# The Strassen output projection of a gated hybrid encoder step: vector and scalar work kept in written order, a third weight slot, six gate buffers

## The chip, the core and the metric

The kernel runs on one core of one Trainium2 chip. The metric is device time in microseconds (us) of one launch. Beside the plain runs stands one profiled execution, whose trace gives every duration below: when each engine started and ended each instruction, and what released it. Engines are named as the profile names them: PE (TensorE matmul) with PEld (its weight loads), DVE (VectorE), ACT (ScalarE), POOL (GpSimd) and SP (the engine that issues the transfers). A "q" behind an engine's name is its sequencer.

## What is computed

One layer of a streaming encoder for 1024 prompt frames and 32 sample frames (1056 columns together, 1024 channels). What matters here is the end of it:

```
ya  = (o_attn * silu(ga)) @ w_pa
yb  = (silu(layernorm(conv)) * silu(gb)) @ w_pb
m   = sigmoid(ma) * ya + sigmoid(mb) * yb
out = x + m @ w_out
```

All products are wanted in full float32. The kernel splits each operand into a rounded high part and the remainder (`wh`, `wl` for weights, `mh`, `ml` for `m`), and adds three matmuls: high by high, low by high, high by low.

## The kernel before

The data lie with channels on the 128 partitions and frames along the free dimension, so a weight of 1024 x 1024 is eight tiles of 128 output channels, each of 8 x 128 x 128 numbers. The program has these stages in order: projections of the input, attention with the gate projections filled in between its blocks, the product with `w_pa` ("pa"), the product with `w_pb` ("pb"), and the output projection with `w_out`.

**A weight** is fetched by `load_raw` (L88, 512 KB, three buffers taken in turn in pa and pb), and split by `split_w`: ACT writes the high part (L94), POOL subtracts it in three pieces to get the low part (L97). `wh` and `wl` have two slots each, in the pool `wp`. One weight feeds 72 matmuls of 352 columns (L105).

**The stage pa** takes, for each of the eight output tiles, three gate tiles `sma` of 352 columns: a transfer reads each (L1173), ACT applies tanh (L1174), DVE multiplies it with the matmul's result from the accumulator (L1177), and a transfer writes it to `s_ya` (L1178). The pool `sg2` has four buffers for them. Between the tiles, `ln_out` (L1127 to L1138) prepares the other branch.

**The stage pb** reads `s_mb` and `s_ya` back, applies tanh (L1215), evaluates (L1220, L1221) and splits `m` (ACT L1224, POOL L1225). In between `form_sums` builds, out of the quarters of `m`, the sums that Strassen's product takes (DVE, L1200 to L1203), and `halves_to` splits them (ACT L1193, DVE L1194).

**The output projection** handles output tiles in four pairs, the frames in two halves of 528 columns (`L`, `R`), and the contraction in two halves of four tiles. Each pair has seven products, each of 24 matmuls of 264 columns (L1290): two in `first`, with the plain weight, and five in `second`, with the weight sums `sa` and `sb` and a plain quarter `z`. All four `first` come before all four `second`. The weight sums are made from two raw weights per pair (DVE L1270, L1271 for `sa`, L1275, L1276 for `sb`, one buffer each) and split by `w_tile` (ACT L1249, POOL L1253, two slots in `wp` and two in `op`). Results leave the accumulator (eight banks, two for a product) by ACT (`u`, L1311) or DVE (`u` L1322, `v` L1325, outputs L1300), are combined with the residual `x` (L1312, L1321), and stored (L1301). The pool `op`, with two of the four weight slots and `tfs[1]`, lies where pb's operands `c_h` and `c_l` lay.

**Order.** From the attention on, only PE keeps the order in which the program is written:

```
es.enter_context(tc.manual_schedule(engines={E.PE}))
```

Instructions of the other engines are ordered by a planner with its own estimate of times, and `tc.high_priority(offset=...)` moves what stands inside ahead. Every engine then works through its list in order, and an instruction that waits holds up all that stand behind it. In the earliest stages DVE and ACT are in the written order too; there `later(n, fn)` puts work at a place n beats ahead, and `beat()` counts a beat and issues what is due.

Of the kernel before, what the change touches and what calls it, by code (L numbers as in the profile page):

```python
# [51 lines left out]
def build(tc, xT, xt, wv, wf, ckT, cv, clT, stT, vec, cst, yT, kT, vO, lfO, cpT, csT):  # L52
# [4 lines left out]
    def pool(name, bufs=1, stack=es, **kw):  # L57
        return stack.enter_context(tc.tile_pool(name=name, bufs=bufs, reuse_waits="tile", **kw))
# [18 lines left out]
    mean = lnp.tile([128, TT], F32, name="mean")  # L77
    rstd = lnp.tile([128, TT], F32, name="rstd")
    rawp = [wp]

    def f32(ap):
        return ap.bitcast(F32)

    def load_raw(key, offset=2000):
        with tc.high_priority(offset=offset):
            rawp.append(rawp.pop(0))
            raw = rawp[-1].tile([128, KT, 128], F32, name="raw", tag="raw", bufs=1)
            nc.sync.dma_start(raw, wf[WIDX[key]])  # L88
        return raw

    def split_w(raw, offset=2000):
        with tc.high_priority(offset=offset):
            wh = wp.tile([128, KT, 128], F32R, name="wh", tag="wh")
            nc.scalar.copy(wh, raw)  # L94
            wl = wp.tile([128, KT, 128], F32R, name="wl", tag="wl")
            for k0, k1 in WSP:
                nc.gpsimd.tensor_sub(wl[:, k0:k1, :], raw[:, k0:k1, :], f32(wh[:, k0:k1, :]))  # L97
        return wh, wl
# [157 lines left out]
    def sums(f):  # L256
        return [lambda: from_shift(f, sides["y", f]), lambda: into_sums(f, sides["y", f])]
# [571 lines left out]
    pps.close()  # L829


    es.enter_context(tc.manual_schedule(engines={E.PE}))
# [355 lines left out]
    L, R = slice(0, HT), slice(HT, TT)  # L1188
    mixed = {}
    parts = {}  # L1190

    def halves_to(h, l, t):
        nc.scalar.copy(h, t)  # L1193
        nc.vector.tensor_sub(l, t, f32(h))  # L1194

    def form_sums(j):
        a, b = mixed.pop(j), mixed.pop(j + 4)
        t, u = (mean, rstd) if j < 3 else (big("t3"), big("u3"))
        V = nc.vector
        V.tensor_sub(t[:, L], a[:, R], a[:, L])  # L1200
        V.tensor_sub(u[:, L], b[:, R], a[:, R])
        V.tensor_sub(t[:, R], b[:, R], t[:, L])
        V.tensor_sub(u[:, R], b[:, L], t[:, R])  # L1203
        halves_to(mh[:, j, R], ml[:, j, R], u[:, L])
        parts[j] = t[:, R], t[:, L], u[:, R]

    def form_halves(j):
        for i, t in enumerate(parts.pop(j)):
            tf = tfs[j // 2]
            halves_to(tf[:, i, 0, j % 2, :], tf[:, i, 1, j % 2, :], t)  # L1210

    def mk_pb(f):
        smb = mixed[f] = big("smb")
# [14 lines left out]
    def formed(f):  # L1228
        for j in range(3):
            if PBO.index(f) == 2 * j + 2:  # L1230
                form_sums(j)
                if j < 2:
                    form_halves(j)
# [5 lines left out]
    rawp.append(op)  # L1239
    tfs.append(op.tile([128, 3, 2, 2, HT], F32R, name="tf"))  # L1240
    homes = [op, op, wp, wp]
    form_halves(2)
    form_sums(3)
    form_halves(3)

    def w_tile(src, n=2):
        homes.append(homes.pop(0))
        wh, wl = [homes[-1].tile([128, KT, 128], F32R, name=a, tag=a, bufs=2) for a in ("wh", "wl")]
        nc.scalar.copy(wh[:, :4 * n, :], src)  # L1249
        for k0, k1 in WSP:  # L1250
            k1 = min(k1, 4 * n)
            if k1 > k0:
                nc.gpsimd.tensor_sub(wl[:, k0:k1, :], src[:, k0:k1, :], f32(wh[:, k0:k1, :]))  # L1253
        return wh, wl

    class Pair:


        def __init__(self, p):
            self.p = p  # L1260
            self.u = op.tile([128, HT], F32, name=f"u{p}")
            self.w = [None] * 3

        def made(self, i):
            V = nc.vector
            with tc.high_priority(offset=2000):
                if i == 0:
                    self.r = [load_raw(("out", 2 * self.p + n), 0) for n in range(2)]
                    sa = self.sa = op.tile([128, KT, 128], F32, name="sa", tag="sa", bufs=1)
                    V.tensor_add(sa[:, 4:, :], self.r[1][:, :4, :], self.r[1][:, 4:, :])  # L1270
                    V.tensor_sub(sa[:, :4, :], sa[:, 4:, :], self.r[0][:, :4, :])  # L1271
                    self.w[0] = w_tile(sa)
                elif i == 1:
                    sb = op.tile([128, KT, 128], F32, name="sb", tag="sb", bufs=1)
                    V.tensor_sub(sb[:, :4, :], self.r[0][:, :4, :], self.r[1][:, :4, :])  # L1275
                    V.tensor_sub(sb[:, 4:, :], self.r[0][:, 4:, :], self.sa[:, :4, :])  # L1276
                    self.w[1] = w_tile(sb)
                else:
                    self.w[2] = w_tile(self.r[1][:, 4:, :], 1)

        def product(self, w, half, mov, evac, pss=None):
            wh, wl = w
            more = pss is not None
            pss = pss or [pjC.tile([128, CH], F32, name="pj", tag="pj") for _ in range(2)]
            for c in range(2):
                for kt in range(4):
                    h, l = [m(kt, slice(c * HC, c * HC + HC)) for m in mov]
                    k = 4 * half + kt
                    for n, (a, x) in enumerate(((wh, h), (wl, h), (wh, l))):
                        nc.tensor.matmul(pss[c][:, :HC], a[:, k, :], x, start=(not more and kt == 0 and n == 0),  # L1290
                                         stop=(kt == 3 and n == 2), skip_group_check=more)
# [15 lines left out]

        def first(self, w, x):
            u = self.u
            self.residual(0, 0, x)  # L1310
            self.product(w, 0, quad(0, L), lambda sl, ps: nc.scalar.copy(u[:, sl], ps))  # L1311
            nc.vector.scalar_tensor_tensor(x, u, 0.5, x, op0=ALU.mult, op1=ALU.add)  # L1312
            self.product(w, 1, quad(4, L), self.out(0, 0, x))

        def second(self, then):
            u, (sa, sb, z) = self.u, self.w
            t1, t2 = big("r1"), big("r2")
            x12, x21, x22, v = t1[:, L], t1[:, R], t2[:, L], t2[:, R]
            for x, m, hf in ((x12, 0, 1), (x21, 1, 0), (x22, 1, 1)):
                self.residual(m, hf, x)  # L1320
            half_of = lambda x, y: nc.vector.scalar_tensor_tensor(y, x, 0.5, y, op0=ALU.mult, op1=ALU.add)  # L1321
            self.product(sa, 0, form(0), lambda sl, ps: nc.vector.tensor_add(u[:, sl], u[:, sl], ps))  # L1322
            half_of(u, x21)
            half_of(u, x12)
            c = self.product(sa, 1, form(1), lambda sl, ps: nc.vector.tensor_add(v[:, sl], u[:, sl], ps))  # L1325
            half_of(v, x22)
            then(0)
            d = self.product(sb, 0, quad(0, R), self.out(1, 1, x22))
            self.product(sb, 1, quad(4, R), self.out(0, 1, x12), c)
            then(1)  # L1330
            self.product(self.w[2], 0, form(2), self.out(1, 0, x21), d)
            then(2)

    def quad(k0, cols):
        return [lambda kt, sl, m=m: m[:, k0 + kt, cols.start + sl.start:cols.start + sl.stop] for m in (mh, ml)]

    def form(i):
        return [lambda kt, sl, n=n: tfs[kt // 2][:, i, n, kt % 2, sl] for n in range(2)]

    pairs = [Pair(p) for p in range(4)]  # L1340
    for p in range(4):
        if p % 2 == 0:
            both = big("r0")
        w = w_next
        if p < 3:
            with tc.high_priority(offset=2000):
                w_next = w_tile(load_raw(("out", 2 * p + 2), 0))
        if p > 1:
            pairs[0].made(p - 2)
        pairs[p].first(w, both[:, (L, R)[p % 2]])  # L1350
    pairs[0].made(2)

    for p in range(4):
        def then(n):
            if n == 0 and p < 3:
                pairs[p + 1].made(0)
            elif n == 1 and p < 3:
                pairs[p + 1].made(1)
            elif n == 2 and p < 3:
                pairs[p + 1].made(2)  # L1360

        pairs[p].second(then)
    p3.close()
    es.close()

# [81 lines left out]
```

## Time and profile before

| what | value |
|---|---|
| runs of the kernel | 1391.44, 1391.41, 1389.38 us; median 1391.41 |
| the profiled execution, its own time | 1390.03 us |
| its span in the trace | 1388.2 us |
| outside the span | 1.8 us |
| mean clock granted to TensorE | 0.999 |
| PE busy | 1374.9 us |
| DVE, ACT, POOL busy | 975.4, 660.0, 653.3 us |

Busy time of PE is that of pipelined matmuls whose ends are modelled: consecutive ones overlap in the record, so their pace is read from their starts. "Idle before, released by" says how long an engine stood still before an instruction and which other engine's instruction ended that.

### The profile page before, as it was taken

The numbers are of one execution on the slowest core, as the hardware profiler recorded it, in microseconds if no ns is written. First come the engines' busy times: TensorE is split into PE (matmuls) and PEld (weight loads), VectorE is DVE, ScalarE is ACT, GpSimd is POOL, SyncE is SP. The second block draws the span as 40 slices with busy tenths as digits, with TensorE's granted clock in tenths as the row PEclk, the third lists the DMA queues.
The fourth block names the chain that finished last, engine by engine and source line by source line (L and its number), as shares of the span: only waits on it lengthen the run. The fifth ranks groups of instructions, "written<-read, shape, count | busy, mean of one in ns | idle before, by whom it ended". The sixth has DMA issues, their size and how long they took to land. (4 is left out here: it accounts for less than half of the span.)

```text
span 1388.2 us, 25134 instructions
## 1 busy us (share of the span) xinstructions
PE 1374.9 (99%) x9478; PEld 1336.3 (96%) x9478; DVE 975.4 (70%) x1368; ACT 660.0 (48%) x1346; POOL 653.3 (47%) x685
## 2 busy tenths in 40 slices
PE   9999999999999999999999999999999999999999
PEld 8999999999999999999999999999999999999999
DVE  6687788878898999647666766655555488156773
ACT  6433434656464642245555556655555566233320
POOL 2324244656575875443433343333433267255662
PEclk9999999999999999999999999999999999999999
DMA  5253442424242374245545556444642678534452
GB/s 213 63 173 123 147 144 92 155 75 160 94 163 88 118 205 152 92 135 136 150 127 164 144 158 178 126 138 139 175 133 88 234 276 272 176 120 144 146 174 69
DMA packets 113496, 203.36 MB, mean 146 GB/s; under 512 B 17696, under 2 KB 75936, under 8 KB 113376
## 3 DMA queue, kind: packets, MB, share of 16 engines
q1 hardware_dynamic: 113232, 201.70, 46.0%
q8 instruction: 75, 1.23, 0.4%
q14 instruction: 45, 0.37, 0.1%
q10 hardware_dynamic: 144, 0.07, 0.0%
HBM read 131.87 MB, written 69.84 MB: 145 GB/s over the span
## 5 line engine op out<-in xcount | busy, mean ns | idle before, releaser
L105 PE MATMUL pj<-xh,wh 128*128 128x352 f32 (+2 forms) x1536 | 509.7, 332 | 0.4 <-ACT t L776 0.3
L105 PE MATMUL pj<-xl,wh 128*128 128x352 f32 (+2 forms) x1536 | 494.9, 322 | 0.2
L105 PE MATMUL pj<-xh,wl 128*128 128x352 f32 (+2 forms) x1536 | 493.5, 321 | 0.0
L97 POOL TENSOR_TENSOR wl<-raw,wh 128x384 fp32r<-128x384 f32 (+1 forms) x237 | 307.5, 1325 | 185.7 <-ACT wh L94 163.2
L269 DVE SCALAR_TENSOR_TENSOR y<-u,vec_t,y 128x1086 f32<-128x1086 f32 x240 | 378.5, 1578 | 11.5 <-ACT y L266 8.3
L105 PEld LDWEIGHTS pj<-xh,wh 128*128 128x128 f32 x1536 | 289.4, 188 | 3.4 <-ACT xh L441 0.9
L105 PEld LDWEIGHTS pj<-xl,wh 128*128 128x128 f32 x1536 | 289.0, 188 | 1.0 <-DVE xl L442 1.0
L105 PEld LDWEIGHTS pj<-xh,wl 128*128 128x128 f32 x1536 | 289.8, 189 | 0.2 <-DVE wl L461 0.2
L954 POOL TENSOR_SCALAR P<-P,nm 128x128 f32<-128x128 f32 (+7 forms) x128 | 99.3, 776 | 230.1 <-DVE nm L953 206.0
L948 DVE TENSOR_REDUCE nm<-psS 128x1 f32<-128x128 f32 (+7 forms) x128 | 96.5, 755 | 72.5 <-PE psS L946 53.8
L975 ACT CAST pth<-ptr 128x512 fp32r<-128x512 f32 (+1 forms) x192 | 89.2, 482 | 80.7 <-PE ptr L971 80.3
L976 DVE TENSOR_TENSOR ptl<-ptr,pth 128x512 fp32r<-128x512 f32 (+1 forms) x192 | 103.4, 551 | 23.3 <-ACT pth L975 21.7
L951 ACT ACTIVATE P<-psS,nm 128x128 f32<-128x128 f32 (+7 forms) x128 | 95.4, 745 | 35.0 <-DVE nm L948 31.4
L94 ACT CAST wh<-raw 128x1024 fp32r<-128x1024 f32 x79 | 82.8, 1048 | 50.7 <-PE pj L105 21.6
L738 POOL TENSOR_TENSOR ql<-qn,qh 128x352 fp32r<-128x352 f32 (+1 forms) x48 | 64.5, 1343 | 68.9 <-ACT qh L737 59.9
L971 PE MATMUL ptr<-ident,P 128*128 128x128 f32 x576 | 85.0, 274 | 0.0
L987 PE MATMUL po<-pth,V 128*128 128x256 f32 x320 | 78.9, 282 | 0.0
L988 PE MATMUL po<-ptl,V 128*128 128x256 f32 x320 | 78.5, 281 | 0.0
L597 PE MATMUL pjv<-vwh,xh 128*128 128x260 f32 x256 | 72.5, 283 | 0.0
L597 PE MATMUL pjv<-vwl,xh 128*128 128x260 f32 x256 | 72.4, 283 | 0.0
L597 PE MATMUL pjv<-vwh,xl 128*128 128x260 f32 x256 | 72.3, 282 | 0.0
L993 DVE TENSOR_TENSOR ot<-ot,po 64x256 f32<-64x256 f32 x64 | 26.7, 417 | 59.7 <-ACT ot L992 59.0
(253 smaller groups left out, 2640.0 us busy)
## 6 DMA issues: line engine op xcount, KB each, us to landing
raw<-wf SPq DMA_DIRECT2D x92, 512.0 KB
s_v<-vb SPq DMA_DIRECT2D x32, 256.0 KB
QB<-s_q SPq DMA_DIRECT2D x32, 256.0 KB
KB<-s_k SPq DMA_DIRECT2D x32, 256.0 KB
V<-s_v SPq DMA_DIRECT2D x16, 512.0 KB
kT<-qn SPq DMA_DIRECT2D x8, 528.0 KB
s_ga<-t SPq DMA_DIRECT2D x24, 176.0 KB
s_gb<-t SPq DMA_DIRECT2D x24, 176.0 KB
```

The source lines that it names most:

```text
L94: nc.scalar.copy(wh, raw)
L97: nc.gpsimd.tensor_sub(wl[:, k0:k1, :], raw[:, k0:k1, :], f32(wh[:, k0:k1, :]))
L105: nc.tensor.matmul(ps, a[:, kt, :], b(kt, sl), start=(first and n == 0), stop=(last and n == N - 1))
L269: t = nc.vector.scalar_tensor_tensor(y, u[:, i:i + CW], w, y, op0=ALU.mult, op1=ALU.add)
L597: nc.tensor.matmul(ps[:, :VC], a, b, start=(n == 0), stop=(n == 23))
L948: nc.vector.tensor_reduce(nm[:, 0:1], ps[:, :nb, :w], axis=AX.XY, op=ALU.max, negate=True)
L951: nc.scalar.activation(P[:, :nk].rearrange("p (b w) -> p b w", b=nb), ps[:, :nb, :w], AF.Exp, bias=nm[:, 0:1], accum_out=nm[:, 1:2])
L954: nc.gpsimd.tensor_scalar(P[:, :nk], P[:, :nk], nm[:, 2:3], 1.0, op0=ALU.mult, op1=ALU.mult)
L971: nc.tensor.transpose(pt[:, 128 * j:128 * j + 128], P[:, 128 * (4 * u + j):128 * (4 * u + j) + 128], ident)
L975: nc.scalar.copy(pth[:, js, qo], p3)
L976: nc.vector.tensor_sub(ptl[:, js, qo], p3, f32(pth[:, js, qo]))
L987: nc.tensor.matmul(po[:, :256], V[:, j, :], pth[:, j, :], start=(j == 0), stop=False)
```

## The change

Two parts. In the stages ahead of the output projection, `sg2` gets six gate buffers, and a new pool `w3` gives a third home to a split weight, so that `split_w` takes `w3`, `wp`, `wp` in turn from the last two gate weights to the end of pa; for pb it is `wp` alone again.

```diff
+    whome = [wp]
...
         with tc.high_priority(offset=offset):
-            wh = wp.tile([128, KT, 128], F32R, name="wh", tag="wh")
+            whome.append(whome.pop(0))
+            home = whome[-1]
+            wh = home.tile([128, KT, 128], F32R, name="wh", tag="wh", bufs=2 if home is wp else 1)
             nc.scalar.copy(wh, raw)
-            wl = wp.tile([128, KT, 128], F32R, name="wl", tag="wl")
+            wl = home.tile([128, KT, 128], F32R, name="wl", tag="wl", bufs=2 if home is wp else 1)
...
-    sg2 = pool("sg2", 4, stack=psg2, side="right")
+    sg2 = pool("sg2", 6, stack=psg2, side="right")
+    whome[:] = [pool("w3", 1, stack=psg2, side="right"), wp, wp]
...
     psg2.close()
+    whome[:] = [wp]
```

In the output projection, PE, DVE and ACT are put in the written order, and the places at which DVE and ACT work is written are given in beats; one beat is three matmuls. The splitting of the sums is broken into single instructions (`third_high`, `third_low`, `form_highs`, `form_low`), and what remained of it after pb goes ahead of, and into, the first product. The number of matmuls, the operations and their shapes are the same.

```diff
-    form_halves(2)
-    form_sums(3)
-    form_halves(3)
+    pe.close()
+    order = ExitStack()
+    order.enter_context(tc.manual_schedule(engines={E.PE, E.DVE, E.Activation}))
...
+        def sums(self, i):
+            r0, r1 = self.r
+            V = nc.vector
+            if i == 0:
+                self.sa = op.tile([128, KT, 128], F32, name="sa", tag="sa", bufs=1)
+                V.tensor_add(self.sa[:, 4:, :], r1[:, :4, :], r1[:, 4:, :])
+            elif i == 1:
+                V.tensor_sub(self.sa[:, :4, :], self.sa[:, 4:, :], r0[:, :4, :])
+            elif i == 2:
+                self.sb = op.tile([128, KT, 128], F32, name="sb", tag="sb", bufs=1)
+                V.tensor_sub(self.sb[:, :4, :], r0[:, :4, :], r1[:, :4, :])
+            else:
+                V.tensor_sub(self.sb[:, 4:, :], r0[:, 4:, :], self.sa[:, :4, :])
...
+        def weights(self, at):
+            for n, fn in zip(at, (self.load, *[lambda i=i: self.sums(i) for i in (0, 1)], lambda: self.made(0),
+                                  *[lambda i=i: self.sums(i) for i in (2, 3)], lambda: self.made(1),
+                                  lambda: self.made(2))):
+                later(n, fn)
...
-                with tc.high_priority(offset=4000):
-                    evac(slice(c * HC, c * HC + HC), pss[c][:, :HC])
+                    if kt == 3:
+                        later(2, lambda cs=cs, ps=pss[c][:, :HC]: evac(cs, ps))
+                    beat()
+                yield
...
+            later(3, lambda: nc.vector.scalar_tensor_tensor(x, u, 0.5, x, op0=ALU.mult, op1=ALU.add))
...
+            later(4, lambda: half_of(u, x21))
+            later(5, lambda: half_of(u, x12))
+            c = yield from self.product(sa, 1, form(1), lambda sl, ps: nc.vector.tensor_add(v[:, sl], u[:, sl], ps))
+            later(3, lambda: half_of(v, x22))
...
+    firsts = [w_next]
+    raws = [load_raw(("out", 2))]
+    both = [big("r0")]
+    for p in range(2):
+        pairs[p].residual(0, 0, both[0][:, (L, R)[p]])
+    form_highs(2)
+    form_sums(3)
+    third_high(3)
+    form_highs(3)
+    for n, (j, i) in enumerate(((2, 0), (2, 1), (2, 2), (3, 0), (3, 1), (3, 2))):
+        later(2 * n, lambda j=j, i=i: form_low(j, i))
+    later(12, lambda: third_low(3))
     for p in range(4):
...
+            later(1, lambda raw=raws.pop(0): firsts.append(w_tile(raw)))
...
+        if p == 2:
+            pairs[0].weights((0, 10, 11, 14, 17, 18, 22, 24))
...
     for p in range(4):
...
+        if p < 3:
+            pairs[p + 1].weights((0, 17, 18, 20, 24, 25, 28, 33))
+        for _ in pairs[p].second():
+            pass
+    while late:
+        beat()
```

More of the change, by code (lines that the diff above doesn't have):

```diff
@@ L829, in build @@
     pps.close()
-    es.enter_context(tc.manual_schedule(engines={E.PE}))
+    pe = ExitStack()
+    pe.enter_context(tc.manual_schedule(engines={E.PE}))
     pace["rate"], pace["credit"] = R_A, 0.0
@@ L1190, in build @@
     parts = {}
-    def halves_to(h, l, t):
-        nc.scalar.copy(h, t)
-        nc.vector.tensor_sub(l, t, f32(h))
     def form_sums(j):
@@ L1203, in form_sums, with third_high, third_low, form_highs @@
         V.tensor_sub(u[:, R], b[:, L], t[:, R])
[L1204 to L1210, printed above, removed]
+        parts[j] = t[:, R], t[:, L], u[:, R], u[:, L]
+    def third_high(j):
+        nc.scalar.copy(mh[:, j, R], parts[j][3])
+    def third_low(j):
+        nc.vector.tensor_sub(ml[:, j, R], parts[j][3], f32(mh[:, j, R]))
+    def form_highs(j):
+        for i, t in enumerate(parts[j][:3]):
+            nc.scalar.copy(tfs[j // 2][:, i, 0, j % 2, :], t)
+    def form_low(j, i):
+        tf = tfs[j // 2]
+        nc.vector.tensor_sub(tf[:, i, 1, j % 2, :], parts[j][i], f32(tf[:, i, 0, j % 2, :]))
     def mk_pb(f):
@@ L1231, in formed @@
                 form_sums(j)
+                third_high(j)
+                third_low(j)
                 if j < 2:
-                    form_halves(j)
+                    form_highs(j)
+                    for i in range(3):
+                        form_low(j, i)
     outproj("pb", lambda kt, sl: ch_[:, kt, sl], lambda kt, sl: cl_[:, kt, sl], mk_pb, formed, PBO)
@@ L1262, in __init__, with load @@
             self.w = [None] * 3
-        def made(self, i):
[L1265 to L1279, printed above, removed]
+        def load(self):
+            self.r = [load_raw(("out", 2 * self.p + n)) for n in range(2)]
+        def sums(self, i):
[11 more added lines that the diff above has]
+                V.tensor_sub(self.sb[:, 4:, :], r0[:, 4:, :], self.sa[:, :4, :])
+        def made(self, i):
+            src = self.r[1][:, 4:, :] if i == 2 else self.sb if i else self.sa
+            self.w[i] = w_tile(src, 1 if i == 2 else 2)
+        def weights(self, at):
[3 more added lines that the diff above has]
+                later(n, fn)
         def product(self, w, half, mov, evac, pss=None):
-            wh, wl = w
             more = pss is not None
@@ L1309, in first, with second @@
             u = self.u
[L1310 to L1316, printed above, removed]
+            yield from self.product(w, 0, quad(0, L), lambda sl, ps: nc.scalar.copy(u[:, sl], ps))
+            later(3, lambda: nc.vector.scalar_tensor_tensor(x, u, 0.5, x, op0=ALU.mult, op1=ALU.add))
+            yield from self.product(w, 1, quad(4, L), self.out(0, 0, x))
+        def second(self):
+            u = self.u
             t1, t2 = big("r1"), big("r2")
             x12, x21, x22, v = t1[:, L], t1[:, R], t2[:, L], t2[:, R]
-            for x, m, hf in ((x12, 0, 1), (x21, 1, 0), (x22, 1, 1)):
+            for x, m, hf in ((x21, 1, 0), (x12, 0, 1), (x22, 1, 1)):
                 self.residual(m, hf, x)
             half_of = lambda x, y: nc.vector.scalar_tensor_tensor(y, x, 0.5, y, op0=ALU.mult, op1=ALU.add)
[L1322 to L1332, printed above, removed]
+            sa, sb, z = [lambda i=i: self.w[i] for i in range(3)]
+            yield from self.product(sa, 0, form(0), lambda sl, ps: nc.vector.tensor_add(u[:, sl], u[:, sl], ps))
+            later(4, lambda: half_of(u, x21))
+            later(5, lambda: half_of(u, x12))
+            c = yield from self.product(sa, 1, form(1), lambda sl, ps: nc.vector.tensor_add(v[:, sl], u[:, sl], ps))
+            later(3, lambda: half_of(v, x22))
+            d = yield from self.product(sb, 0, quad(0, R), self.out(1, 1, x22))
+            yield from self.product(sb, 1, quad(4, R), self.out(0, 1, x12), c)
+            yield from self.product(z, 0, form(2), self.out(1, 0, x21), d)
     def quad(k0, cols):
@@ L1340, in build @@
     pairs = [Pair(p) for p in range(4)]
+    firsts = [w_next]
[10 more added lines that the diff above has]
+    later(12, lambda: third_low(3))
     for p in range(4):
-        if p % 2 == 0:
-            both = big("r0")
-        w = w_next
         if p < 3:
[L1346 to L1351, printed above, removed]
-    for p in range(4):
[L1354 to L1362, printed above, removed]
+            later(1, lambda raw=raws.pop(0): firsts.append(w_tile(raw)))
+        if p < 2:
+            raws.append(load_raw(("out", 2 * p + 4)))
+        if p == 1:
+            both.append(big("r0"))
+            for n in range(2):
+                pairs[2 + n].residual(0, 0, both[1][:, (L, R)[n]])
+        if p == 2:
+            pairs[0].weights((0, 10, 11, 14, 17, 18, 22, 24))
+        for _ in pairs[p].first(lambda p=p: firsts[p], both[p // 2][:, (L, R)[p % 2]]):
+            pass
+    for p in range(4):
+        if p < 3:
+            pairs[p + 1].weights((0, 17, 18, 20, 24, 25, 28, 33))
+        for _ in pairs[p].second():
+            pass
+    while late:
+        beat()
+    order.close()
     p3.close()
```

4 lines of the change are left out of this document (3 added, 1 removed).

## The prediction

> **What bounds the kernel now.** I read the busy shares first, then what PE waited for.
>
> ```profile
> PE 1374.9 (99%) x9478; PEld 1336.3 (96%) x9478; DVE 975.4 (70%) x1368; ACT 660.0 (48%) x1346; POOL 653.3 (47%) x685
> ...
> PE pj L1290 <- DVE r L1325: 2.6, 1, 2.6
> PE pj L105 <- ACT wh L94: 2.1, 1, 2.1
> PE pj L1290 <- DVE r L1300: 0.7, 1, 0.7
> PE pj L105 <- POOL wl L97: 0.7, 1, 0.7
> ```
>
> The lower four lines are all waits of PE after 1050 us (total, times, longest). PE is the bound, the change leaves its 9478 matmuls as they are, so only waits can be won: 2.6 + 2.1 + 0.7 + 0.7 = 6.1 us. A matmul of 264 columns is recorded as lasting 284 ns, but 408 of them took 50.03 us, 123 ns each (row below); a gap in the record therefore hides some 0.16 us of lost pace. Four gaps: 6.1 + 4 x 0.16 = **6.8 us**, half in pa (3.1), half in the output projection (3.7).
>
> The pa gap, first by SP, then ACT, POOL and PE:
>
> ```profile
> 1182.83 0.99 SPq L1178 DMA_DIRECT2D s_ya<-sma  x2
> 1190.72 0.80 SPq L1173 DMA_DIRECT2D sma<-s_ma  x2
> ...
> SPq L1173 <- DMA s_ya<-sma: 20.6, 8, 6.9
> ...
> 1188.99 1.09 ACT L1215 ACTIVATE smb<-smb 128x1056 f32<-128x1056 f32 x1 [4.88 <-DMA smb<-s_mb]
> 1193.02 0.50 ACT L1174 ACTIVATE sma<-sma 128x352 f32<-128x352 f32 x1 [2.94 <-DMA sma<-s_ma]
> 1193.43 1.03 ACT L94 CAST wh<-raw 128x1024 fp32r<-128x1024 f32 x1
> 1194.59 2.67 POOL L97 TENSOR_TENSOR wl<-raw,wh 128x384 fp32r<-128x384 f32 x3 [12.67 <-issue]
> 1194.51 0.42 PE L105 MATMUL pj<-ah,wh 128*128 128x352 f32 x1 [2.10 <-ACT wh L94]
> 1200.00:1250.00 50.00, 50.00 (x313) 50.00 (x312) 22.36 (x34) 14.53 (x22) 24.38 (x23) 1.00 0.42 138
> ```
>
> A gate tile's load waited 6.9 us until the store out of the same buffer had landed; the tanh waited for the load; and the next weight's cast, 1 us of work, stood behind the tanh on an ACT that had been idle. It is an order fault, not a lack of ACT time. The last row (PE's 313 matmuls in 50 us) gives 0.16 us a matmul, 11.5 us a weight.
>
> The output projection's two gaps, by DVE and the chain of waits:
>
> ```profile
> 1313.23 1.43 DVE L1275 TENSOR_TENSOR sb<-raw 128x512 f32<-128x512 f32 x1
> ...
> 1317.04 0.76 DVE L1300 SCALAR_TENSOR_TENSOR r<-pj,r 128x264 f32<-128x264 f32 x2
> ...
> 1327.81 5.92 DMA raw<-wf
> ...
> 1333.85 0.09 DVE sa L1270
> ...
> 1334.52 0.43 DVE r L1325
> ...
> 1335.00 50.03 PE pj L1290 x408
> ...
> 1385.05 0.43 DVE r L1300
> ```
>
> At 1333.85 DVE added raw weights that had just landed; the evacuation `v` (L1325), for which PE waited, stood behind it. These were sums for pair 2: of the 672 matmuls 264 were done, 192 of them `first`, so PE was still 24 x 2 matmuls short of the end of pair 0. The planner had put them a whole pair too early. The smaller gap is alike: L1275 ran before the output evacuation L1300. After 1335 PE never waits.
>
> **The change, part by part.**
>
> *Six gate buffers.* Three tiles make a weight, so two more buffers give a load 2/3 x 11.5 = 7.7 us more until its buffer's store must have landed; the longest wait was 6.9. Cost: two 176 KB loads stand ahead of pa's first operands.
>
> ```profile
> 1100.00:1150.00 50.00, 50.00 (x311) 50.00 (x311) 39.47 (x33) 32.91 (x38) 28.53 (x16) 1.00 0.84 300
> 1110.46 0.33 PE L105 MATMUL pj<-ah,wh 128*128 128x352 f32 x1
> 1115.31 1.75 DVE L1121 TENSOR_TENSOR al<-a,ah 128x1056 fp32r<-128x1056 f32 x1 [0.93 <-ACT ah L1120]
> ```
>
> At the 300 GB/s of that stretch they take 1.2 us. The last operand was ready at 1115.31 + 1.75 = 1117.1; PE, nine matmuls a contraction tile, needs it 7 x 1.44 us after 1110.46, at 1120.5. The 3.4 us of cover hold; past them each us costs one.
>
> *Third weight slot.* A split weight can be begun two weights (23 us) before its use instead of one. The late cast then has its slot a weight earlier, and it was 2.1 us late. Either half of this part would nearly do. I count the full **-3.1 us**. A loss is possible only by planner's reshuffling; bounds 0 and -3.1.
>
> *Written order in `second`.* `sums` of the next pair now stand at beats 17, 18, 24, 25 of the pair before, `v` at 14 and 18; PE wants `v` at 24 and 28. One beat is 3 x 0.123 = 0.37 us. The weight needed at beat 40 is cast at 20: 1.05 us on ACT and (next rows) 2.7 to 4.1 on POOL are at most 14 beats. The slots it takes were last read at beat 0, 16 or 32 by PE, its cast stands behind those, so ACT does not block. The raw loads stand at beat 0, two of four buffers, 6.3 us ahead of the sums at a landing time of 5.92, and SP may issue them earlier. Both gaps go: **-3.7 us**. SP keeps its stores and residual loads, and the planner orders it as before.
>
> *The start of the projection.* Here something is lost.
>
> ```profile
> 1299.16 0.29 PE L1290 MATMUL pj<-mh,wh 128*128 128x264 f32 x1
> 1299.36 2.95 ACT L1249 CAST wh<-raw 128x1024 fp32r<-128x1024 f32 x3 [2.21 <-PE pj L105]
> 1303.29 0.63 ACT L1193 CAST tf<-rstd 128x528 fp32r<-128x528 f32 x1
> 1303.82 0.64 ACT L1193 CAST tf<-t 128x528 fp32r<-128x528 f32 x1
> 1304.35 0.49 ACT L1224 CAST mh<-smb 128x352 fp32r<-128x352 f32 x1
> 1300.49 12.27 POOL L1253 TENSOR_TENSOR wl<-raw,wh 128x384 fp32r<-128x384 f32 x9 [2.32 <-ACT wh L1249]
> 1342.41 2.68 POOL L1253 TENSOR_TENSOR wl<-sa,wh 128x384 fp32r<-128x384 f32 x3 [1.92 <-ACT wh L1249]
> 1299.92 0.53 DVE L1221 TENSOR_TENSOR smb<-smb,ya 128x352 f32<-128x352 f32 x1
> 1300.48 0.71 DVE L1201 TENSOR_TENSOR u<-smb 128x528 f32<-128x528 f32 x1
> ```
>
> Before, ACT cast three weights the moment PE let go of pb's operands (1299.36), and POOL followed. Now pair 1's weight stands at beat 1, behind seven casts of 528 columns (three of `form_highs(2)`, `third_high(3)`, three of `form_highs(3)`), which start no earlier: `tfs[1]` lies in the same memory. PE needs that weight after two products, 48 matmuls: 1299.16 + 5.9 = 1305.0. Casts start 0.53 apart. If `form_highs(2)` goes first, the seven and the 352-column one (0.4) end at 1299.36 + 7 x 0.53 + 0.4 = 1303.5; DVE's four sums, now with POOL idle, end near 1300.45 + 4 x 0.65 = 1303.0, so the last cast ends at 1303.6. Weight cast 1.05, first POOL piece 1.07: 1305.7, a wait of 0.6. If the 352-column cast comes first, which waits for L1221, the seven end at 1304.6, the first piece by 1306.7 to 1307.0 (1.07 alone, 1.36 beside DVE), and the second piece may lag 0.3: a wait up to 2.3. Bounds 0 (a planner that still casts early) and 2.3; I take the middle of the two orders, **+1.5 us**. Later weights follow in time: POOL ends the second by 1313, when PE needs its first piece done, the third by 1317, needed at 1318.8.
>
> The waiting of ACT holds up pair 0's two `u` evacuations; they free two of eight banks, and PE fills two per 2.9 us, so there is room until about 1311. DVE's seven subtractions hold up the output evacuations alike: at 1.4 each, as L1275 took beside POOL above, seven from 1303 on end at 1313, as late as before.
>
> Does the new wait cost clock as well? Two waits of PE, by their windows' granted clock (the column ahead of the DMA share):
>
> ```profile
> 19.52 0.89 PE L439 MATMUL ptx<-ident,xtok 128*128 128x128 f32 x3 [1.48 <-DVE xl L442]
> ...
> 18.00:20.00 2.00, 0.52 (x4) 0.48 (x4) 2.00 (x5) 0.00 (x0) 1.63 (x2) 0.89 1.01 410
> 20.00:22.00 2.00, 2.00 (x12) 2.00 (x11) 1.63 (x4) 1.56 (x3) 0.00 (x0) 0.50 0.69 230
> 22.00:24.00 2.00, 2.00 (x14) 2.00 (x13) 1.76 (x4) 1.70 (x5) 0.00 (x0) 0.76 0.00 0
> ...
> 1300.00:1350.00 50.00, 46.66 (x382) 46.24 (x381) 42.48 (x59) 16.33 (x27) 35.38 (x31) 1.00 0.63 204
> ```
>
> Behind 1.48 us of waiting at the start of the program, where PE had been thinly used, the clock was halved; behind 2.60 us at 1332, after dense work, it stayed at 1.00. The new wait is of the second kind, so I add nothing, and keep the drop as rival 4. The Trainium skill ("TensorE: Matmul & The Clock Gate", Part 1: The HAM clock gate) says that PE falls to half its clock after at least one idle window of about 3.4 us and needs as long a busy one to return. Taken as bare idle time, that rule excludes a drop here as well, but the trace's drop behind 1.48 us speaks against such a threshold.
>
> *Sum.* -3.1 - 3.7 + 1.5 = -5.3. The profiled execution took 1390.03, below the median 1391.41 and above the fastest, 1389.38; the four average 1390.57. 1390.57 - 5.3 = **1385.3 us**. The end (evacuation, last store, from 1385.05 to 1388.2) stays.
>
> **The rivals.**
>
> 1. *No new wait* (0.14): ACT or the planner finishes pair 1's weight in time. 1390.6 - 6.8 = 1383.8; from the fastest run 1382.6. For it: DVE sums ran at 0.6 to 0.7 alone. Against: the chain above has no slack in either order.
>
> 2. *pa keeps its gap* (0.13): transfers, at 0.84 of their engines, are the true limit, and the planner orders ACT behind another load (it waited 4.9 us for `smb` too). 1390.6 - 3.7 + 1.5 = 1388.4. Against: that weight's raw copy was asked for at 1157.28, 36 us before the cast, so only order held it.
>
> ```profile
> 1157.28 0.37 SPq L88 DMA_DIRECT2D raw<-wf  x1
> ```
>
> 3. *DVE blocked in written order: slower* (0.12). The planner could slip an evacuation past a late raw weight; the written order can't. `v`'s second half stands behind `sums(1)`, and PE wants it at beat 28, 10.3 us into `second`. With 5.92 for the landing, two sums of 0.7 and 0.43 for `v`, it decides at an issue later than 10.3 - 5.92 - 1.4 - 0.4 = 2.6 us after beat 0, as when SP stands behind a store. At SP's longest wait, 6.9, each of three pairs loses 4.3 us: +12.9 - 5.3, 1398. Against: the buffers come free a pair earlier, and before, a load (row below) went out at 1313.93 for pair 1, whose sums would now be due past 1329.
>
> ```profile
> 1313.93 0.38 SPq L88 DMA_DIRECT2D raw<-wf  x1
> ```
>
> 4. *The clock drops at the start of the projection* (0.08). By the three windows above the drop at 20 us took 2 x (0.11 + 0.50 + 0.24) = 1.7 us of PE's pace. Added to the 1.5 at pair 1: 1385.3 + 1.7 = 1387.0. For it: the new wait is as long as that one. Against: none of the four waits after 1050, up to 2.6 us, did it.
>
> 5. *It doesn't do what it says* (0.05): waits merely move; 1390.6.
>
> **How the numbers follow.** Forecast 0.48. What a measurement here can tell from no change is 0.2%, 2.8 us, so the line is 1388.6. Faster: forecast, rival 1, nearly half of rival 2: 0.48 + 0.14 + 0.06, and rival 4, 0.08: 0.76. Within: the rest of 2, and 5: 0.12. Slower: rival 3, 0.12. The range runs from rival 1 in a run as fast as the fastest (1382.6, less 0.2 for their spread) to rival 2 in a run like the median, 1.0 above its 1388.4: 1389.4. It leaves out rivals 3 and 5, 0.17.
>
> **What would show it.** PE's list of waits after 1050 without L94, L97, L1325 and L1300; in their place one wait of 0.6 to 2.3 us at about 1302 on the new cast or its POOL piece, six microseconds into the projection. SP's wait of `sma` loads on `s_ya` stores should shrink from 20.6, and the weight casts in pa should lead their use by over 10 us. The prediction is wrong if PE waits in pa remain, if a wait recurs once a pair on DVE, or if the start costs over 2.3.

## The result, and the profile after

| | before | after |
|---|---|---|
| median of six runs, us | 1391.19 (1389.38 to 1391.44) | 1384.49 (1384.09 to 1385.52) |
| the profiled execution, us | 1390.03 | 1384.38 |
| its span, us | 1388.2 | 1382.3 |
| its last matmul starts at, us | 1384.73 | 1378.82 |

The ratio of the times is 0.9955, with a 95% interval of 0.9942 to 0.9968. The forecast was 1385.3 in a range of 1382.4 to 1389.4.

The difference of these medians, 6.7 us, rests on six executions of the kernel before that came out longer than others of it. On three other occasions, 65 executions in all, the kernel before had a median of 1389.79 us, and against that the kernel after is 5.3 us faster. Why the six were longer is not known: their granted clocks are not on record.

The busy shares after, then all the waits of PE between 1050 and 1383 us (total, times, longest):

```profile
PE 1372.3 (99%) x9478; PEld 1333.4 (96%) x9478; DVE 975.5 (71%) x1368; ACT 659.0 (48%) x1346; POOL 654.7 (47%) x685
```

```profile
PE pj L108 <- ACT t L779: 1.1, 1, 1.1
PE pj L1315 <- POOL wl L1267: 0.7, 1, 0.7
```

The four waits of before (6.1 us) are gone: no weight cast, no output evacuation and no `v` is waited for any more. The second of the two new ones was forecast. The first was not, and it stands in a stage of which the prediction says nothing.

The last links of the chain that ended last (start, length, what):

```profile
1088.27 203.88 PE pj L108 x1272
...
1301.57 2.47 POOL wl L1267 x2
1304.08 75.03 PE pj L1315 x614
```

From 1088 to 1292, through pa and nearly all of pb, PE is its own predecessor, and after the start of the projection it is so once more to the end.

Busy shares don't show where the time went; the start of each stage on PE does. A stage begins where its first matmul starts. Three such starts in the trace of after, read by the operand's name (`ah` for pa, `c_h` for pb) or the line (L1315 for the projection):

```profile
1111.09 0.33 PE L108 MATMUL pj<-ah,wh 128*128 128x352 f32 x1
...
1204.12 0.32 PE L108 MATMUL pj<-c_h,wh 128*128 128x352 f32 x1
...
1295.79 0.29 PE L1315 MATMUL pj<-mh,wh 128*128 128x264 f32 x1
```

The lengths by these starts, to the start of the last matmul:

| stretch | before | after | difference |
|---|---|---|---|
| up to the first matmul of 352 columns | 48.23 | 47.50 | -0.73 |
| to 1045 us | 996.78 | 996.88 | +0.10 |
| end of the attention, 1045 to 1088 us | 42.42 | 43.61 | **+1.19** |
| to the first matmul of pa | 23.03 | 23.10 | +0.07 |
| pa | 96.81 | 93.03 | **-3.78** |
| pb | 91.89 | 91.67 | -0.22 |
| output projection | 85.57 | 83.03 | **-2.54** |
| sum | | | -5.91 |

The second row differs by more than that among executions (996.77 to 997.38 in the twelve traces of this document), so its +0.10 says nothing.

**pa.** SP's wait for gate stores is down from 20.6 us to 11.3, and the last weight of pa is cast 14 us ahead of its use at about 1192.5:

```profile
SPq L1178 <- DMA s_ya<-sma: 11.3, 8, 5.4
```

```profile
1178.11 1.04 ACT L97 CAST wh<-raw 128x1024 fp32r<-128x1024 f32 x1
...
1188.74 1.09 ACT L1225 ACTIVATE smb<-smb 128x1056 f32<-128x1056 f32 x1 [4.18 <-DMA smb<-s_mb]
1189.73 1.03 ACT L97 CAST wh<-raw 128x1024 fp32r<-128x1024 f32 x1
```

The last two rows show that the fault itself is still there: a cast stands behind a tanh that waits 4.18 us for a transfer. It is now a weight of pb, wanted at 1204, so nothing is lost.

**The start of the projection**, on ACT, POOL and PE:

```profile
1295.83 1.17 ACT L1216 CAST tf<-mean 128x528 fp32r<-128x528 f32 x2 [2.06 <-PE pj L108]
...
1299.90 0.64 ACT L1216 CAST tf<-u 128x528 fp32r<-128x528 f32 x1 [0.20 <-DVE u L1205]
1300.44 1.05 ACT L1263 CAST wh<-raw 128x1024 fp32r<-128x1024 f32 x1
```

```profile
1302.64 0.39 PE L1315 MATMUL pj<-mh,wl 128*128 128x264 f32 x1 [0.71 <-POOL wl L1267]
```

Pair 1's weight is cast behind the seven casts of the sums, which begin when PE lets go of pb's operands at 1295.8; its first POOL piece, begun at 1301.57 (chain above), ends at 1302.6. PE stood for 0.71 us there and, counted by starts, lost 1.4 (worked out below).

**The wait at 1050**, on ACT, first before, then after:

```profile
1049.62 0.43 ACT L776 COPY t<-pj 128x352 f32<-128x352 f32 x1
...
1064.54 1.05 ACT L94 CAST wh<-raw 128x1024 fp32r<-128x1024 f32 x1
```

```profile
1048.48 1.05 ACT L97 CAST wh<-raw 128x1024 fp32r<-128x1024 f32 x1 [1.31 <-DMA raw<-wf]
...
1050.19 0.43 ACT L779 COPY t<-pj 128x352 f32<-128x352 f32 x1
```

The third home of a weight is free here, so the planner casts the last gate weight but one at once (before: at 1064.54), while its raw copy is still under way. ACT waits 1.31 us at the cast, and the evacuation `t` that PE wants stands behind it: from the start of this stretch on PE (1045.01 before, 1044.38 after) it begins 4.61 us in before and 5.81 us in after, 1.2 later. It is the fault that the change mends in pa, made anew 140 us earlier.

### The profile page after: what moved, and what is told of

It reads as the page before. It is cut to its first block, busy times and chain, and to the rows that moved or that the text cites. A ratio compares the mean times of both kernels' runs of the same rounds, so it can differ in the third digit from the quotient of the medians.

```text
span 1382.3 us, 25127 instructions
## 1 busy us (share of the span) xinstructions
PE 1372.3 (99%) x9478; PEld 1333.4 (96%) x9478; DVE 975.5 (71%) x1368; ACT 659.0 (48%) x1346; POOL 654.7 (47%) x685
## 4 chain that ended last, share of the span: by engine, by line
PE 95%; DMA 1%; DVE 1%; ACT 1%; issue 1%; POOL 0%; SPq 0%; ACTq 0%; POOLq 0%; DVEq 0%
PE pj L108 65%; PE pjv L600 7%; PE pj L1315 5%; PE ptr L975 5%; PE po L991 3%; PE po L992 3%; PE psS L947 3%; PE psS L948 2%; DMA xtok<-xt 1%; PE psS L950 1%; PE pst L724 1%; PE pst L723 1%; DMA raw<-wf 0%; PE ptx L442 0%; DMA u<-stT 0%
## 5 line engine op out<-in xcount | busy, mean ns | idle before, releaser
L100 POOL TENSOR_TENSOR wl<-raw,wh 128x384 fp32r<-128x384 f32 (+1 forms) x237 | 311.0, 1340 | 184.6 <-ACT wh L97 165.0
```

## The experiments

The ledger of all kernels, by the same starts. The last column is the time against the kernel before, measured beside it, with its 95% interval.

| kernel | end of attention | pa | projection | median us, before's beside it | ratio |
|---|---|---|---|---|---|
| before | 42.42 | 96.81 | 85.57 | | |
| after | 43.61 | 93.03 | 83.03 | 1384.49, 1391.19 | 0.9955 (0.9942 to 0.9968) |
| `six_buffers` | 42.42 | 94.52 | 85.63 | 1388.45, 1389.5 | 0.9988 (0.998 to 0.9997) |
| `third_slot` | 42.42 | 93.02 | 87.50 | 1391.29, 1389.5 | 1.0006 (0.9997 to 1.0015) |
| `written_order` | 42.41 | 97.43 | 83.03 | 1385.97, 1389.5 | 0.998 (0.9971 to 0.9988) |
| `sums_no_priority` | 42.42 | 96.13 | 88.45 | 1391.14, 1389.5 | 1.0011 (1.0 to 1.0022) |
| `part_one` | 43.31 | 93.03 | 87.09 | 1388.1, 1389.85 | 0.9984 (0.9976 to 0.9993) |
| `third_slot_deeper` | 43.34 | 93.02 | 87.77 | 1388.07, 1389.85 | 0.9989 (0.998 to 0.9998) |
| `cast_first` | 43.49 | 93.03 | 81.66 | 1382.99, 1390.03 | 0.9951 (0.9939 to 0.9964) |
| `slot_from_pa` | 42.45 | 92.99 | 83.05 | 1383.91, 1390.03 | 0.9958 (0.9945 to 0.997) |
| `cast_first_slot_from_pa` | 42.42 | 93.00 | 81.66 | 1382.34, 1390.03 | 0.9948 (0.9934 to 0.9962) |
| `two_raw_buffers` | 42.41 | 93.00 | 96.30 | 1396.11, 1389.85 | 1.0045 (1.0031 to 1.0059) |

**`six_buffers`**: the kernel before with the gate buffers alone.

```diff
-    sg2 = pool("sg2", 4, stack=psg2, side="right")
+    sg2 = pool("sg2", 6, stack=psg2, side="right")
```

> The kernel before with six gate buffers and nothing else. Theory A (the gap of pa came from gate loads waiting for the stores out of the same buffer; either half of the first part would nearly do): the waits of 2.1 and 0.7 us at 1194 go, the output projection keeps its 2.6 and 0.7, no new wait near 1050; 1391.2 - 3.3 = about 1388. Rival B (the late cast needs the third slot): the gap at 1194 stays, 1391.

PE's waits after 1050 in that kernel, and what stood ahead of the late cast on ACT:

```profile
PE pj L1290 <- DVE r L1325: 2.7, 1, 2.7
...
PE pj L105 <- POOL wl L97: 0.7, 1, 0.7
```

```profile
1189.12 1.09 ACT L1215 ACTIVATE smb<-smb 128x1056 f32<-128x1056 f32 x1 [5.88 <-DMA smb<-s_mb]
...
1190.76 1.03 ACT L94 CAST wh<-raw 128x1024 fp32r<-128x1024 f32 x1
```

The cast came 2.7 us earlier than in before (1193.43), and 2.3 of pa's 3.8 us went. The rest stayed: the cast now stood behind the tanh of `smb`, whose load ACT awaited for 5.88 us. More gate buffers do nothing for that load. This is rival 2's mechanism, at less than half its size: 1.5 us of pa's loss are left, of which the starts around the wait show 1.1. The other 0.45 has another cause, given in the last section.

**`third_slot`**: the kernel before with the third home alone, four gate buffers.

```diff
+    whome = [wp]
...
+            whome.append(whome.pop(0))
+            home = whome[-1]
+            wh = home.tile([128, KT, 128], F32R, name="wh", tag="wh", bufs=2 if home is wp else 1)
...
+    whome[:] = [pool("w3", 1, stack=psg2, side="right"), wp, wp]
```

> The kernel before with the third home for split weights and four gate buffers. Theory A: the cast of pa's last weight moves a weight ahead, the gap at 1194 goes, but the wait of 1.1 us near 1050, seen after the change, appears, because the weight of the last gates but one is then cast inside the attention and the evacuation of a gate stands behind the cast: 1391.2 - 3.3 + 1.2 = about 1389. Rival B (the gap needs the buffers): wait near 1050 and a gap in pa both, 1391 to 1392. Rival C (the wait near 1050 comes from another part of the change): 1388 with none near 1050.

```profile
PE pj L108 <- ACT wh L97: 1.5, 1, 1.5
...
PE pj L108 <- POOL wl L100: 0.7, 1, 0.7
```

```profile
1086.96 0.36 ACT L995 COPY ot<-po 64x256 f32<-64x256 f32 x1 [1.53 <-PE po L991]
1087.35 1.05 ACT L97 CAST wh<-raw 128x1024 fp32r<-128x1024 f32 x1
```

pa runs without a gap (93.02 us), yet the kernel gains nothing. The same two waits, 1.5 and 0.7 us, now stand at 1087, ahead of the last gate weight but one, and the stretch from there to pa takes 25.8 us instead of 23.0. Its cast came only behind the attention's last output (`ot`), 23 us later than in before. Two readings were open: the planner chose it so, or the third home lies in memory that the attention's last tiles still hold.

**`third_slot_deeper`** tells these apart: still four gate buffers, but an otherwise unused tile of the size of two of them lies ahead of the third home, so that this has the address that it has in after.

```diff
     sg2 = pool("sg2", 4, stack=psg2, side="right")
+    pad = pool("pad", 1, stack=psg2, side="right").tile([128, 2 * CH], F32, name="pad")
+    nc.gpsimd.memset(pad[:, 0:1], 0.0)
+    whome[:] = [pool("w3", 1, stack=psg2, side="right"), wp, wp]
```

> The third home with four gate buffers, and an unused tile of two gate buffers' size ahead of it, so that it lies where it lies after the change. Theory (with four gate buffers the third home begins on memory that the attention's last tiles still hold, so the first weight put there is cast only at 1087 and PE waits 1.5 and 0.7 for it): that gap goes, the cast moves back to about 1048 with the wait of 1.1 near 1050, pa stays without a gap; 0.2% below the kernel before. Rival (the planner's order, or the number of gate buffers, decides): the gap at 1087 stays and the time is that of the kernel before.

```profile
PE pj L108 <- ACT t L779: 0.9, 1, 0.9
```

```profile
1048.76 1.05 ACT L97 CAST wh<-raw 128x1024 fp32r<-128x1024 f32 x1 [1.05 <-DMA raw<-wf]
```

It was the address. The cast is back at 1048.76, the wait at 1087 is gone, the one near 1050 is there, and pa has no gap with four gate buffers. So the six buffers in after are needed for where they push the third home, not for the loads of `sma`.

**`part_one`**: the kernel before with both halves of the first part.

> The change's first part alone: six gate buffers and the third home. If the parts add up: no PE wait in pa (its 576 matmuls in 93.0 us instead of 96.8), a wait of 1.1 near 1050 (1.2 lost), the projection's waits of 2.6 and 0.7 unchanged: 0.27% below the kernel before, some 1387. If the wait near 1050 needs the second part, 1386.

```profile
PE pj L1295 <- DVE r L1330: 2.6, 1, 2.6
PE pj L108 <- ACT t L779: 0.8, 1, 0.8
PE pj L1295 <- DVE r L1305: 0.7, 1, 0.7
```

pa as in after; the wait near 1050 (0.8 us) comes with this part; the projection keeps both of its waits.

**`written_order`**: the second part alone, that is after with four gate buffers and no third home.

> The change's second part alone: the output projection in the written order, four gate buffers and two weight slots. Theory A: the gap of pa (2.1 and 0.7) stays, the projection's 2.6 and 0.7 go, one wait of 0.7 comes on the POOL piece of pair 1's weight, 1.3 in matmul starts with its train; 1391.2 - 3.7 + 1.3 = about 1388.8. Rival: if the two parts need each other, no gain, 1391.

```profile
PE pj L108 <- ACT wh L97: 1.2, 1, 1.2
PE pj L1314 <- POOL wl L1266: 0.7, 1, 0.7
PE pj L108 <- POOL wl L100: 0.7, 1, 0.7
```

The projection takes the 83.03 us that it takes in after, with the same wait at its start; pa keeps its gap. The two parts are independent: against the kernel before measured beside each, this one is 3.5 us faster and `part_one` 1.8, together 5.3, which is what the whole change gains against the 65 executions named above. That pa is 0.6 us longer than in before though its waits are shorter (1.9 us against 2.8) is taken up below.

**`sums_no_priority`**: the kernel before, with the raised priority taken off the instructions that split the sums (`made`).

```diff
-            with tc.high_priority(offset=2000):
+            with tc.high_priority(offset=0):
```

> The kernel before, where only the priority of 2000 ahead of the weight sums of the second products is taken away, DVE and ACT still ordered by the planner. If that priority alone put the sums of pair 2 too early (rival to the need of a written order), the projection's waits of 2.6 and 0.7 go and nothing is lost at the start: 1391.2 - 3.7 = 1387.5. If the planner's estimate is at fault, waits of like size stay or come elsewhere, 1390 to 1393.

```profile
PE pj L1290 <- DVE r L1325: 2.8, 1, 2.8
```

The wait stays, and so does the one of 0.7 us on L1300. It is not that priority which put the sums ahead of the evacuations in before; the planner's own order did.

**`cast_first`**: after, with pair 1's weight cast ahead of the casts of the sums.

```diff
+    firsts.append(w_tile(raws.pop(0)))
     form_highs(2)
...
-        if p < 3:
+        if 0 < p < 3:
             later(1, lambda raw=raws.pop(0): firsts.append(w_tile(raw)))
```

> The kernel after the change, with pair 1's weight cast written ahead of the casts of the sums instead of behind them. Theory (the wait of 0.7 at 1302, 1.3 us in matmul starts, is that cast's place in ACT's list): the wait goes, PE has none in the projection, 1384.5 - 1.3 = 1383.2. Rival (POOL or DVE is the limit there; POOL and DVE then slow each other sooner): part of it stays or moves to the second or third weight, 1384 to 1385.

PE waits nowhere in the projection, which takes 81.66 us. That is the length without any gap, and it prices the others: the new wait in after cost 83.03 - 81.66 = 1.4 us, and the two gaps of before 85.57 - 81.66 = 3.9.

**`slot_from_pa`**: after, with the third home taken into the turn only from pa on.

```diff
-    whome[:] = [pool("w3", 1, stack=psg2, side="right"), wp, wp]
+    w3 = pool("w3", 1, stack=psg2, side="right")
...
+    whome[:] = [w3, wp, wp]
```

> The kernel after the change, with the third home taken into turn only from the first weight of pa, not from the last two gate weights on. Theory: the wait of 1.1 us near 1050 goes, pa still has none: 1384.5 - 1.2 = 1383.3. Rival (the early turn is what gives pa its lead): a wait returns in pa, 1384 to 1387.

The wait near 1050 is gone (42.45 us for the end of the attention, as before), and pa still has no gap.

**`cast_first_slot_from_pa`**: both edits together.

> Both of the edits at once. If the two waits are independent, 1384.5 - 1.3 - 1.2 = 1382.0, and PE waits for nothing from 1000 us on. If the planner reshuffles, one of the waits remains, about 1383.3.

The last link of its chain:

```profile
1294.82 81.79 PE pj L1316 x672
```

All 672 matmuls of the projection are one link, and PE waits for nothing after 1000 us. It is the fastest version: 1382.34 us, 7.7 less than the kernel before beside it.

**`two_raw_buffers`**: that kernel with two buffers for raw weights in the projection instead of four, to see whether the written order can be held up as rival 3 said.

```diff
-    rawp.append(op)
+    rawp.pop()
```

> The kernel with pair 1's cast first and the third home from pa on, and two raw weight buffers in place of four in the output projection, so that a pair's loads can't go out before the pair ahead has read its own. It tries the slower rival of the prediction: a late raw weight would block DVE's evacuations in the written order, once a pair, with a PE wait on L1349, L1327 or their like, by up to 4 us a pair, 1390 and above. Against it: by the beats the buffers come free 3 to 15 beats ahead of the next pair's begin and land by beat 14, ahead of the sums at 17: no PE wait, 0.55% below the kernel before as without the edit; pair 1's or 2's plain weight may come late by 1 us.

```profile
PE pj L1316 <- ACT wh L1264: 4.0, 1, 4.0
PE pj L1316 <- DVE r L1353: 3.3, 2, 2.6
```

SP, and then DVE, around these waits:

```profile
1330.48 1.57 SPq L89 DMA_DIRECT2D raw<-wf  x1
```

```profile
1335.33 0.69 DVE L1287 TENSOR_TENSOR sa<-raw 128x512 f32<-128x512 f32 x1 [3.97 <-DMA raw<-wf]
1335.94 0.42 DVE L1353 TENSOR_TENSOR r<-u,pj 128x264 f32<-128x264 f32 x1
...
1354.06 0.69 DVE L1287 TENSOR_TENSOR sa<-raw 128x512 f32<-128x512 f32 x1 [6.70 <-DMA raw<-wf]
```

My expectation of no cost was wrong. A raw weight asked for at 1330.48, 8.5 us after `second` began at 1322.01, held DVE for 3.97 us, and the evacuation for which PE waited (L1353) stood behind the sum. Here PE waited 0.70 us; at the same beat of the next pair, where DVE stood for 6.70 us (last row), it waited 2.63. The longest wait, 4.0, is on pair 0's own split sum, which was cast late because DVE had stood 7.57 us for the raw weight of that sum. The projection lost 14.6 us against the version with four buffers: 9.3 of recorded waits (two more rows, of 1.1 and 0.9 us, are not shown but counted), and most of the rest in clock, as follows.

**What a wait costs besides itself.** Two things in the ledger don't fit waits alone: the long pa of `written_order`, and projections of 87.1 to 88.5 us in kernels whose waits there are those of before, within 0.7 us (longest 2.6 to 3.3). The granted clock (third number from the end) explains both. Before, behind its wait of 2.60 us; `six_buffers`, behind 2.70; `part_one`, behind 2.62; `sums_no_priority`, behind 2.79:

```profile
1336.00:1338.00 2.00, 2.00 (x18) 2.00 (x18) 1.90 (x4) 0.00 (x0) 0.00 (x0) 1.00 0.66 243
```

```profile
1334.00:1336.00 2.00, 2.00 (x18) 2.00 (x18) 1.90 (x6) 0.27 (x1) 0.00 (x0) 1.00 0.63 228
```

```profile
1330.00:1332.00 2.00, 0.17 (x1) 0.18 (x2) 1.74 (x3) 0.00 (x0) 0.88 (x2) 0.96 0.08 8
1332.00:1334.00 2.00, 2.00 (x10) 2.00 (x11) 1.86 (x5) 0.00 (x0) 0.00 (x0) 0.50 0.78 266
1334.00:1336.00 2.00, 2.00 (x13) 2.00 (x13) 1.87 (x4) 0.00 (x0) 0.00 (x0) 0.69 0.40 135
```

```profile
1334.00:1336.00 2.00, 1.20 (x5) 1.20 (x6) 1.97 (x5) 0.00 (x0) 0.00 (x0) 0.51 0.20 30
1336.00:1338.00 2.00, 2.00 (x11) 2.00 (x10) 1.90 (x5) 0.00 (x0) 0.00 (x0) 0.50 0.69 262
1338.00:1340.00 2.00, 2.00 (x11) 2.00 (x10) 0.85 (x2) 0.00 (x0) 0.00 (x0) 0.50 0.34 114
1340.00:1342.00 2.00, 2.00 (x16) 2.00 (x14) 0.43 (x1) 0.62 (x1) 0.68 (x1) 0.78 0.80 194
```

The same wait, of nearly the same length, was followed by full clock in two executions and by half clock in two others. The clock missing in `part_one` is 2 x (0.04 + 0.50 + 0.31) = 1.7 us, that in `sums_no_priority` 2 x (0.49 + 0.50 + 0.50 + 0.22) = 3.4. So half clock lasted 3.4 us or twice that. In `written_order` it came behind the waits of 1.2 and 0.7 us in pa:

```profile
1194.00:1196.00 2.00, 1.56 (x8) 1.56 (x9) 0.21 (x1) 0.50 (x1) 2.00 (x3) 0.89 0.27 85
1196.00:1198.00 2.00, 2.00 (x8) 2.00 (x8) 0.00 (x0) 0.00 (x0) 0.04 (x1) 0.50 0.36 68
1198.00:1200.00 2.00, 2.00 (x12) 2.00 (x11) 0.00 (x0) 0.00 (x0) 0.00 (x0) 0.76 0.78 285
```

That is 1.7 us again, which accounts for its long pa: 97.43 - 1.7 is 95.7, shorter than before's. `third_slot` and `third_slot_deeper` lost about 1.7 each in the same way, `two_raw_buffers` 3.4 behind the wait of 4.0 and 1.7 behind that of 2.6. It shows across executions too. Of 65 executions of the kernel before whose clock is on record, the 22 with a mean granted clock of 1.000 have a median of 1388.53 us, the 18 with 0.999 one of 1389.77, the 14 with 0.998 one of 1390.83, the 7 with 0.997 one of 1391.7, the 4 with 0.996 one of 1393.3. All 65 lie between 1386.76 and 1394.02 us, standard deviation 1.5; the five of `cast_first_slot_from_pa` between 1381.74 and 1382.99, deviation 0.5.

The Trainium skill ("TensorE: Matmul & The Clock Gate", Part 1: The HAM clock gate) gives the window in which activity is judged as 3.4 us, free-running, and one busy window as the way back to full clock. The 1.7 and 3.4 us of lost clock, one and two such windows at half pace, agree with it. The same section of the Trainium skill puts half clock behind at least one idle window of that length. Read as bare idle time, that does not agree: here waits of 1.2 and 0.7 us in a row were followed by half clock in one execution, and a single wait of 2.62 in another.

## Why the prediction came out right, step by step

- **What bounds the kernel**: right. PE's work stayed, and only waits were won. All four forecast to go went.
- **pa, -3.1**: right in mechanism, 0.7 too small: -3.8. 3.3 of it is the two gaps by the starts of the matmuls on either side. The other 0.45 was not foreseen: three of pa's eight weights lie in the third home, and PE goes through each of these 0.15 us faster (last section). The size of the gaps differs among executions: in `sums_no_priority`, whose edit does not touch pa, it is 2.7, and pa 96.13 us, 3.1 longer than in after.
- **"Either half of this part would nearly do"**: half right. Six buffers alone left a wait of 0.7 us and 1.5 us of pa's loss, by rival 2's mechanism. The third home alone does all of it in pa, but at the address that four gate buffers give it, it sent the same loss to 1087 us. What the buffers were for was misread.
- **"A loss is possible only by planner's reshuffling; bounds 0 and -3.1"**: incomplete. The loss was named and given no price; -3.8 and +1.2 together stay inside the bounds. The third home cost 1.2 us at the end of the attention, since a free slot invites an early cast, and a cast ahead of its raw data holds up ACT. `slot_from_pa`, where it is taken up later and the wait is absent, shows that this is its doing.
- **Two 176 KB loads ahead of pa's operands, no cost**: right; PE did not wait at pa's start.
- **Written order, -3.7**: right, 3.9 by `cast_first`. Neither `sums` nor `v` was late in any pair.
- **Start of the projection, +1.5 (0 to 2.3)**: the chain went as written, with `form_highs(2)` first, and the wait of 0.71 us is the 0.6 forecast for that order. That the cost, +1.4, meets the forecast of +1.5 is luck: the 1.5 was the middle between this order and one that did not come. The sum for this order had left out PE's lost pace, which the prediction itself puts at 0.16 us a gap, and the next POOL piece, for which PE was held up again (two starts 0.37 us apart instead of 0.12).
- **No clock lost at the new wait**: true of the profiled execution. But the reason against rival 4, that none of the four waits of before had cost clock, was one execution's luck; in `part_one` the same wait of 2.6 us did cost it. Nor does it help that PE had worked densely ahead of the wait, by which the prediction told this wait from the one at 20 us. A wait removed takes with it the clock that it sometimes cost; how much of the measured gain is due to this was not separated.
- **Rival 3**, slower by a late raw weight: real with two raw buffers, and absent with four. The place was right, beat 28 of `second`, and the size was not: for an issue 8.5 us after beat 0 the estimate gives a wait of 8.5 - 2.6 = 5.9 us, and PE waited 0.70. PE itself came to that beat 3.4 us late, held up by its earlier waits and half clock; the raw weight was there 4.85 us after its issue, not 5.92; and one sum, not two, stood ahead of the evacuation. The bound of 2.6 was not tried.
- **The sum**: -5.3 forecast, -5.9 by the starts of the two traces, with two terms outside it that partly cancel: +1.2 near 1050, and -0.7 in the first 48 us. The latter is no part of the change: both executions wait 1.48 us at 19.5 us, but the clock behind it fell to 0.50 in before and stayed at 1.00 in after. Of the twelve traces only one other, `sums_no_priority`, shows that drop, and these two take 48.2 us there, the ten others 47.3 to 47.7. Without the two terms, the rest comes to -3.78 - 2.54 - 0.22 + 0.17 = -6.4, against -5.3. So the total came so near because a cost that the forecast had not priced stood against a gain that it had too small.

## What to carry to other kernels

An instruction that waits for a transfer on an engine that also evacuates the accumulator is the first suspect when PE waits for an engine that is half idle; look at what stands ahead of the late one, not at the load of the engine. A new buffer lets its writer run earlier, so ask where that writer will then stand and whether its data are there; and where the buffer lies decides which older tile it must wait for. When the bound engine waits, the price is the wait and now and then 1.7 or 3.4 us of clock (here behind a single wait of 1.5 us and more, or two of 1.2 and 0.7 in a row), so one profiled execution without the drop is no evidence that there is none.

## What the runs showed of the hardware that was not expected

- The clock behind a PE wait of the same place and length differs among executions: 2.62 us was followed by 0.50, 2.70 us by 1.00; the loss came in steps of 1.7 us.
- PE's pace follows the place of the weight. The first matmuls of pa's fifth, sixth and seventh weight in after:

```profile
1157.70 0.32 PE L108 MATMUL pj<-ah,wh 128*128 128x352 f32 x1
...
1169.22 0.32 PE L108 MATMUL pj<-ah,wh 128*128 128x352 f32 x1
...
1180.93 0.32 PE L108 MATMUL pj<-ah,wh 128*128 128x352 f32 x1
```

The fifth, which lies in the third home, took 11.53 us for its 72 matmuls, the sixth, in `wp`, 11.70. All of pa goes like that: 11.50 to 11.53 for the second, fifth and eighth weight, 11.66 to 11.74 for the others. In `slot_from_pa`, where the turn begins at pa, it is the first, fourth and seventh that take 11.52 and 11.53, and in before, without a third home, no weight takes less than 11.67. The transfers do not explain it: their share was 0.76 during the fifth weight and 0.77 during the sixth. In pb, with the same shapes and weights in `wp` again, a weight takes 11.45 us from the third on, so the place of the weight is not all that counts; why it counts was not tried.
